# Packing the experts' leftover tokens four to a block instead of two in a mixture-of-experts layer

## The chip, the cores and the metric

The kernel runs on one core of one Trainium2 chip. The metric is the device time of one execution in microseconds (us): the median of several runs.

## What is computed

One decoder layer over 1024 tokens of width 1024, in float32: a mixer (a convolution group and a gated group, between two projections), LayerNorm, a two-level mixture of experts (MoE), and a gated LayerNorm. What the change touches is the MoE:

```python
g_p, g_idx = lax.top_k(g_probs, 1)                    # one of 4 groups
e_p, e_idx = lax.top_k(softmax(e_logits), 2)          # two of its 4 experts
expert_ids = g_idx * EXPERTS_PER_GROUP + e_idx
hidden = silu(x @ w_gate[e]) * (x @ w_up[e]) * combine[:, e]
y = sum over e of hidden @ w_down[e]
```

There are 16 experts, each with 1024 x 256 gate and up weights and 256 x 1024 down weights: 3 MB an expert. Each token goes to two experts, so there are 2048 (token, expert) pairs. With the inputs of the reference the experts get, in order, 88, 15, 27, 62, 451, 602, 461, 264, 17, 19, 10, 2, 13, 1, 9 and 7 tokens.

## The kernel before

**Stages.** The input projection and the convolutions come first, then the output projection with LayerNorm and the router (`choose`, `rank`: which expert, and which place in it, each token has), then a stretch in which the tokens are sorted into blocks, then the expert loop (line 1400), then the gate and the last LayerNorm (line 1485). Almost all multiplications split their operands into a high and a low part and run three passes (`mm3`). The order of work on every engine is written by hand (`manual_schedule`): what a queue is given first, it does first.

**Blocks.** An expert's tokens fill whole blocks of 128 rows; of what is left, over 64 tokens get a whole block too, and 1 to 64 get a half (`H` = 64 rows). With the counts above there are 16 whole blocks (1, 4, 5, 4 and 2 of experts 0, 4, 5, 6 and 7) and 12 rests of 64 rows. Blocks 0 to 15 (`NA`) are whole. Blocks 16 to 21 (up to `NS` = 22) hold two rests side by side, those of two experts: rest j takes columns 64j to 64j+63 of the array. These pair blocks run in plain float32, without the split. Blocks 22 and 23 run only where there are more rests than that (`plain_block`, in an `If`).

**Index work.** Lines 1143 to 1222, on VectorE, work out for every token its block and its row in it (`bf`, `qf`), make one-hot matrices `oh` (row, POOL, line 686) and `ohb` (block and half, line 1199), and one chain of small matmuls (line 1210) gives `idx`, the token for each row of each block. The expert of each unit goes into `ebi`, which SP reads as registers (`expert`, line 756).

**The loop** runs b = 0 to 13. Pass b multiplies whole block b+1 by gate and up (`gate_up`, two halves of 12 matmuls), turns block b+2 (`turn`), does block b's `down` (12 matmuls), splits the weights of block b+2 (ACT and DVE) and issues the loads for block b+3 on SP; these are conditional and move nothing when the block has the same expert (`changed`). Of the whole blocks that follow, 5, 10 and 14 have another expert than the one before.

**Pair steps** lie between these parts, one after each half of `gate_up` (from b = 1) and one or two (`EXTRA`) after `down`. A pair block has eight: `turn_plain`; four `pair_gu`; `pair_hid`; two `pair_down`. The six with weights issue four matmuls on 64 array columns each, 512 wide; the trace shows each as two records, so a weight step is eight records of 128 x 64 x 512. It reads two tiles of 512 KB, one of each expert.

**The ring** holds these tiles: four slots of two tiles. `load_pair` fills it, in the order of use: four slots ahead before the loop (line 1397), and after each weight step two tiles for the slot that the step has freed (`load_some`). They are issued on SP without condition, between the loads of the whole blocks and the stores of results (`store_y`), and SP takes all of these in order. The pool `rp` has 7 buffers: two for the down weights, two of the ring, the rest for `y`. Tokens are gathered by POOL.

Of the kernel before, what the change touches and what calls it, by code (L numbers as in the profile page):

```python
# [12 lines left out]
I32 = mybir.dt.int32  # L13
# [20 lines left out]
H = P // 2  # L34
NA = 16
NS = 22
# [9 lines left out]
def decoder_layer(ctx: ExitStack, tc: tile.TileContext, t: dict, out: bass.AP):  # L46
# [13 lines left out]
    rp = ctx.enter_context(tc.tile_pool(name="rp", bufs=7))  # L60
# [444 lines left out]
    pidx_m = const.tile([P, 1], F32, name="pidx_m")  # L505
    nc.gpsimd.iota(pidx_m, pattern=[[0, 1]], base=-1000, channel_multiplier=1, allow_small_or_imprecise_dtypes=True)
# [146 lines left out]
    def rank(t0, t1, weave=()):  # L653
# [16 lines left out]
        for step in (  # L670
# [4 lines left out]
            lambda: nc.vector.tensor_single_scalar(ri, si, 6, op=OP.logical_shift_right),  # L675
# [3 lines left out]
            next(weave, lambda: None)()  # L679
            step()  # L680
# [86 lines left out]
    def changed(b):  # L767
        return {"cond": expert(2 * b) != expert(2 * b - 2)} if b else {}

    def load_gu(b, part=range(4)):  # L770
        for q in part:
            fetch_gu(raw[q], expert(2 * b), q, **changed(b))

    def load_d(b):
        for k in range(2):
            fetch_d(rdn[k], expert(2 * b), k, **changed(b))
# [159 lines left out]
    def pair_gu(s, q):  # L936
# [3 lines left out]
        for k in range(2):  # L940
            for j in range(2):
                c = (2 * q + k) * P + j * H
                nc.tensor.matmul(pgu[b][j * H:(j + 1) * H, :], xgT[b][:, c:c + H],  # L943
                                 ring[(6 * s + q) % len(ring)][j].rearrange("p (m k f) -> p k m f", m=2, k=2)[:, k, :, :],
                                 start=q + k == 0, stop=q + k == 4)
# [3 lines left out]
    def pair_hid(s):  # L949
# [5 lines left out]
    def pair_down(s, k):  # L955
# [3 lines left out]
        for h in range(2):  # L959
            for j in range(2):  # L960
                c = k * P + j * H
                nc.tensor.matmul(pdn[b][h][j * H:(j + 1) * H, :], hTp[b][:, c:c + H],  # L962
                                 ring[(6 * s + 4 + k) % len(ring)][j][:, h * 512:(h + 1) * 512], start=k == 0, stop=k == 1)
# [3 lines left out]
    def plain_block(b):  # L967
        w4 = [*ring[0], *ring[1]]
        w4k = [a.rearrange("p (m k f) -> p m k f", k=2, m=2) for a in w4]
        src, xT = ring[2]  # L970
        gather(b, src)
        turn_plain(b, xT)
        for j in range(2):
            e = nc.sync.value_load(ebi[0:1, 2 * b + j:2 * b + j + 1], min_val=0, max_val=NE - 1)
# [66 lines left out]
    oh = line("oh")[:, 0:NT * H].bitcast(F16).rearrange("p (j t q) -> p j t q", j=2, q=H)  # L1041
# [83 lines left out]
    for h in range(2):  # L1125
# [24 lines left out]
        lambda: nc.vector.scalar_tensor_tensor(ci, count[0], float(H - 1), floor_, op0=OP.add, op1=OP.max),  # L1150
# [4 lines left out]
        lambda: nc.vector.tensor_scalar(odd0, pairs, -1.0, float(2 * NA), op0=OP.mult, op1=OP.add),  # L1155
        lambda: nc.vector.tensor_max(odd0, odd0, pairs),
# [9 lines left out]
    nc.vector.tensor_scalar(own[:, 0, :], cx[:, 0:NE], 2.0, pidx, op0=OP.mult, op1=OP.is_le)  # L1166
    nc.vector.scalar_tensor_tensor(wk, cs[:, 0:NE], -2.0, uo, op0=OP.mult, op1=OP.add)
    nc.vector.tensor_scalar(own[:, 1, :], cs[:, 0:NE], 2.0, pidx, op0=OP.mult, op1=OP.is_gt)
    nc.vector.scalar_tensor_tensor(wk, wk, 32.0, nf[:, 0:NE], op0=OP.mult, op1=OP.add)
    nc.vector.scalar_tensor_tensor(own[:, 2, :], nf[:, NE:], -1000.0, uo, op0=OP.mult, op1=OP.add)  # L1170
# [5 lines left out]
    nc.vector.scalar_tensor_tensor(own[:, 0, :], own[:, 2, :], pidx_m, own[:, 0, :], op0=OP.is_equal, op1=OP.add)  # L1176
# [13 lines left out]
    nc.vector.scalar_tensor_tensor(wf[:, 1, :], wf[:, 1, :], 2.0, hb, op0=OP.mult, op1=OP.is_le)  # L1190
    nc.vector.scalar_tensor_tensor(bf, wf[:, 0, :], 2.0, hb, op0=OP.mult, op1=OP.add)
# [5 lines left out]
    ebi = const.tile([1, 64], I32, name="ebi")  # L1197
    ohb = ebx[:, 256:256 + NT * 2 * NB].bitcast(F16).rearrange("p (c l b) -> p c l b", l=2, b=NB)
    nc.vector.tensor_tensor(
        ohb, iorow[:, 0:2 * NB].rearrange("p (b l) -> p l b", l=2)[:, None, :, :].to_broadcast([P, 2 * NT, 2, NB]),  # L1200
        bf[:, :, None, None].to_broadcast([P, 2 * NT, 2, NB]), op=OP.is_equal)
    nc.vector.tensor_copy(ebi[:, 0:2 * NB], pe[0:1, 0:2 * NB])
# [4 lines left out]
    todo = [(j, i) for i in range(NT) for j in range(2)]  # L1207
    for n, (j, i) in enumerate(todo):
        for l in range(2):
            ahead = nc.tensor.matmul(pix[l * H:(l + 1) * H, 0:NB], oh[:, j, i, :], ohb[:, j * NT + i, l, :],  # L1210
# [5 lines left out]
    nc.vector.tensor_scalar(ebi[:, 63:64], cs[0:1, 2 * NE - 1:2 * NE], odd0[0:1, :], None, op0=OP.add)  # L1216
# [346 lines left out]
```

## Time and profile before

| | |
|---|---|
| median of 3 runs | 733.39 us (732.62 to 735.53) |
| profiled execution, own time | 732.19 us |
| its span, first to last instruction | 730.4 us |
| TensorE matmuls (PE) busy | 708.3 us, 97% |
| VectorE (DVE), ScalarE (ACT), GpSimd (POOL) busy | 564.0, 332.4, 184.9 us |
| moved by DMA | 142.09 MB |

The loop with pair steps lies between about 403 and 604 us of the span. PE, DVE, ACT and POOL are engines; "PEld" is the loading of PE's weights; "SPq" is SP issuing a transfer. "gu" and "dn" are the outputs of gate/up and of down, "gT" a turned block, "hT" turned hidden values, "cv" and "rdn" the tiles that receive a whole block's weights, "ring" those of the rests. Line numbers are those of the kernel before.

### The profile page before, as it was taken

What the parts mean: (1) busy time and instruction counts of PE and PEld (TensorE: products, weight loads), DVE (VectorE), ACT (ScalarE), POOL (GpSimd) and SP (SyncE); (2) the same over time, 40 slices, a digit from 0 to 9 for tenths busy, and PEclk for the clock granted to TensorE, in tenths of its full rate; (3) what the DMA queues carried; (4) which work ended last, traced back from release to release, by engine and by line L of the source; (5) the groups of instructions that cost most, each with busy time, mean ns of one, the idle gap of its engine ahead of it and who ended that gap; (6) DMA issues with size and microseconds to landing.
All of it is one profiled execution on the core that took longest, in us unless ns stands there. A gap on an engine that the chain in (4) does not pass through costs nothing.

```text
span 730.4 us, 10338 instructions
## 1 busy us (share of the span) xinstructions
PE 708.3 (97%) x3558; PEld 537.3 (74%) x3558; DVE 564.0 (77%) x790; ACT 332.4 (46%) x544; POOL 184.9 (25%) x174
## 2 busy tenths in 40 slices
PE   6999999999999999999989999999999999999995
PEld 5898888888888888777767565665665666787874
DVE  6958999997985788998767656866556576788786
ACT  5761112324223733450357676767565675522220
POOL 3262122456363212135251110111011101621101
PEclk9999999999999999999999999999999999999999
DMA  8554111110111313452267899988888976887422
GB/s 311 207 210 156 57 57 35 54 57 30 58 58 51 123 58 116 139 179 87 116 235 272 329 402 387 358 310 322 301 331 318 385 257 238 280 305 243 173 90 84
DMA packets 40283, 142.09 MB, mean 195 GB/s; under 512 B 4610, under 2 KB 4738, under 8 KB 40228
## 3 DMA queue, kind: packets, MB, share of 16 engines
q1 hardware_dynamic: 33412, 116.95, 43.7%
q0 software_dynamic: 6672, 24.25, 9.6%
q8 instruction: 29, 0.48, 0.3%
q14 instruction: 26, 0.21, 0.1%
q10 hardware_dynamic: 144, 0.20, 0.1%
HBM read 149.77 MB, written 26.21 MB: 241 GB/s over the span
## 4 chain that ended last, share of the span: by engine, by line
PE 85%; DVE 5%; DMA 3%; issue 2%; POOL 2%; ACT 2%; SPq 0%; DVEq 0%; POOLq 0%; ACTq 0%
PE gu L943 6%; PE gu L94 4%; PE gu L96 4%; PE gu L95 4%; PE mix L555 4%; PE pg L1307 3%; PE mix L556 3%; PE mix L559 3%; PE pg L1308 3%; PE pg L1311 3%; PE dn L962 3%; PE gT L818 2%; PE c L263 2%; PE v L260 2%; PE v L259 2%
## 5 line engine op out<-in xcount | busy, mean ns | idle before, releaser
L283 DVE SCALAR_TENSOR_TENSOR cacc<-ab,tapT,cacc 128x1024 f32<-128x1024 f32 x116 | 149.6, 1290 | 10.9 <-ACT cacc L280 7.1
L91 DVE TENSOR_TENSOR el<-cv,eh 128x1024 fp32r<-128x1024 f32 x63 | 74.3, 1221 | 24.1 <-ACT eh L90 23.3
L143 POOL TENSOR_TENSOR wl<-wr,wh 128x1024 fp32r<-128x1024 f32 (+1 forms) x25 | 47.9, 1927 | 97.2 <-ACT wh L140 97.2
L809 POOL DMA_INDIRECT xg<-x_d,idx x22 | 25.7, 1170 | 178.1 <-PE gT L818 125.0
L140 ACT CAST wh<-wr 128x1024 fp32r<-128x1024 f32 x20 | 21.1, 1053 | 107.3 <-issue 35.0
L90 ACT CAST eh<-cv 128x1024 fp32r<-128x1024 f32 x63 | 62.9, 1052 | 0.0
L94 PE MATMUL gu<-eh,gh 128*128 128x512 f32 x128 | 53.2, 416 | 0.2 <-ACT gh L90 0.2
L555 PE MATMUL mix<-woh,ah 128*128 128x512 f32 x128 | 52.8, 413 | 0.0
L96 PE MATMUL gu<-eh,gl 128*128 128x512 f32 x128 | 50.2, 392 | 0.0
L556 PE MATMUL mix<-wol,ah 128*128 128x512 f32 x128 | 50.2, 392 | 0.0
L95 PE MATMUL gu<-el,gh 128*128 128x512 f32 x128 | 50.2, 392 | 0.0
L1307 PE MATMUL pg<-wgh,rh 128*128 128x512 f32 x120 | 48.2, 402 | 0.0
L1308 PE MATMUL pg<-wgl,rh 128*128 128x512 f32 x120 | 46.9, 391 | 0.1
L943 PE MATMUL gu<-ring,gx 128*64 128x512 f32 x192 | 45.6, 603 | 0.0
L187 POOL TENSOR_TENSOR rs<-ve,mhalf 128x1 f32<-128x1 f32 x16 | 17.4, 1090 | 95.9 <-DVE ve L186 95.9
L91 DVE TENSOR_TENSOR gl<-gT,gh 128x512 fp32r<-128x512 f32 x32 | 20.6, 685 | 26.7 <-ACT gh L90 26.7
L559 PE MATMUL mix<-woh,al 128*128 128x512 f32 x128 | 40.9, 390 | 0.0
L91 DVE TENSOR_TENSOR dl<-rdn,dh 128x1024 fp32r<-128x1024 f32 x32 | 37.8, 1220 | 2.6 <-ACT dh L90 1.3
L1311 PE MATMUL pg<-wgh,rl 128*128 128x512 f32 x120 | 37.7, 390 | 0.0
L90 ACT CAST dh<-rdn 128x1024 fp32r<-128x1024 f32 x32 | 32.2, 1060 | 0.0
L94 PEld LDWEIGHTS gu<-eh,gh 128*128 128x128 f32 x128 | 24.1, 188 | 11.1 <-issue 4.1
L259 PE MATMUL val<-xh,wh 128*128 128x256 f32 (+1 forms) x88 | 30.4, 346 | 0.0
(315 smaller groups left out, 1770.5 us busy)
## 6 DMA issues: line engine op xcount, KB each, us to landing
cv<-in_w_gu SPq DMA_DIRECT2D x60, 512.0 KB
ring<-in_w_gu SPq DMA_DIRECT2D x48, 512.0 KB
rdn<-in_w_down SPq DMA_DIRECT2D x32, 512.0 KB
ring<-in_w_down SPq DMA_DIRECT2D x24, 512.0 KB
ys_d<-y SPq DMA_DIRECT2D x22, 512.0 KB
wr<-in_w_in SPq DMA_DIRECT2D x20, 512.0 KB
wor<-in_w_out SPq DMA_DIRECT2D x8, 512.0 KB
y<-in_x SPq DMA_DIRECT2D x8, 512.0 KB
```

The costliest lines, as they stand in the source:

```text
L90: nc.scalar.copy(hi, src)
L91: (eng or nc.vector).tensor_sub(lo, src, hi.bitcast(F32))
L94: nc.tensor.matmul(o, ah, bh, start=start, stop=False)
L95: nc.tensor.matmul(o, ah, bl, start=False, stop=False)
L96: nc.tensor.matmul(o, al, bh, start=False, stop=stop)
L283: nc.vector.scalar_tensor_tensor(dst, abuf[c][:, j:j + SEQ], w, cacc[c], op0=OP.mult, op1=OP.add)
L555: nc.tensor.matmul(pmix[i][h], hi[:, ks], wh[:, s], start=k == 0, stop=False)
L556: nc.tensor.matmul(pmix[i][h], hi[:, ks], wl[:, s], start=False, stop=False)
L559: nc.tensor.matmul(pmix[i][h], lo[:, ks], wh[:, s], start=False, stop=k == NK - 1)
L943: nc.tensor.matmul(pgu[b][j * H:(j + 1) * H, :], xgT[b][:, c:c + H], ring[(6 * s + q) % len(ring)][j].rearrange("p (m k f) -> p k m f", m= ...
L1307: nc.tensor.matmul(pgt[i][h], hi[:, ks], wh[:, s], start=False, stop=False)
L1308: nc.tensor.matmul(pgt[i][h], hi[:, ks], wl[:, s], start=False, stop=False)
```

## The change

Rests come in units of 32 rows. An expert's rest of 1 to 32 tokens is one unit, of 33 to 64 two units of the same expert (over 64 a whole block, as before). Four units lie side by side in a block, 32 columns each, and there are four such blocks (16 to 19) for six; 20 to 23 stand in the `If`. The four units' tiles make a weight step of sixteen records of 128 x 32 x 512, which reads four tiles of 512 KB. The ring has ten single tiles (four of them now from `rp`, which gets 8 buffers), and after a weight step four loads are issued. A load of the ring carries the condition that the unit is in use. Index arithmetic changes accordingly; `ohb` becomes two arrays of 768 columns, one for each of a token's two choices, and the chain for `idx` has 64 matmuls of 32 columns for 32 of 64. `EXTRA` has six entries for nine and adds one step, not a second one, after `down`. Two more blocks of zeros are stored early. POOL's descriptor space is halved.

```diff
-H = P // 2
-NS = 22
+H = P // 4
+L = P // H
+NS = 20
-    rp = ctx.enter_context(tc.tile_pool(name="rp", bufs=7))
+    rp = ctx.enter_context(tc.tile_pool(name="rp", bufs=8))
...
-    def load_pair(s, n):
-        for j in range(2):
-            to, e = ring[(6 * s + n) % len(ring)][j], expert(2 * (NA + s) + j)
-            if n < 4:
-                fetch_gu(to, e, n)
-            else:
-                fetch_d(to, e, n - 4)
+    def held(s, n, j):
+        return ring[(L * (6 * s + n) + j) % len(ring)]
+
+    def load_quad(s, n, j):
+        u = L * (NA + s) + j
+        (fetch_gu if n < 4 else fetch_d)(held(s, n, j), expert(u), n % 4, cond=used > u)
...
-            for j in range(2):
+            for j in range(L):
                 c = (2 * q + k) * P + j * H
                 nc.tensor.matmul(pgu[b][j * H:(j + 1) * H, :], xgT[b][:, c:c + H],
...
-        lambda: nc.vector.tensor_scalar(ni[:, 1, :], ci, 6, 1, op0=OP.logical_shift_right, op1=OP.bitwise_and),
+        lambda: nc.vector.tensor_scalar(ni[:, 1, :], ci, 5, 3, op0=OP.logical_shift_right, op1=OP.bitwise_and),
         lambda: nc.vector.tensor_copy(nf, ni.rearrange("p a e -> p (a e)")),
+        lambda: nc.vector.tensor_scalar(nf[:, NE:], nf[:, NE:], 1.0, -1.0, op0=OP.max, op1=OP.add),
...
+    nc.vector.tensor_add(own[:, 0, :], own[:, 0, :], own[:, 2, :])
...
+    for j in range(2):
+        nc.vector.tensor_tensor(
+            ohb[j], iorow[:, 0:L * NB].rearrange("p (b l) -> p l b", l=L)[:, None, :, :].to_broadcast([P, NT, L, NB]),
+            bf[:, j * NT:(j + 1) * NT, None, None].to_broadcast([P, NT, L, NB]), op=OP.is_equal)
+        if j == 0:
+            nc.vector.tensor_copy(ebi[:, 0:L * NB], pe[0:1, 0:L * NB])
...
-    ring.append([line(f"ring{j}")[:, 0:D] for j in range(2)])
-    ring.extend([wide("ring", 2 * n + j)[:, 0:D] for j in range(2)] for n in range(2))
-    ring.append([R(f"ring{j}") for j in range(2, 4)])
+    ring.extend(line(f"ring{j}")[:, 0:D] for j in range(2))
+    ring.extend(wide("ring", j)[:, 0:D] for j in range(4))
+    ring.extend(R(f"ring{j}") for j in range(4))
...
-        for _ in range(done[0]):
+        for _ in range(L * done[0]):
             if loads:
-                load_pair(*loads.pop(0))
+                load_quad(*loads.pop(0))
...
-    EXTRA = (1, 2, 3, 4, 9, 10, 11, 12, 13)
+    EXTRA = (1, 3, 5, 7, 9, 11)
...
-        pair_some(2 if b in EXTRA else 1)
+        quad_some(1 if b in EXTRA else 0)
         load_some()
...
-    nc = _bacc.Bacc("TRN2", target_bir_lowering=False, num_devices=1)
+    nc = _bacc.Bacc("TRN2", target_bir_lowering=False, num_devices=1, dynamic_dma_scratch_size=8192)
```

## Rows read from the trace of the kernel before

**Rows 1.** The page: busy time of each engine over the span.
```profile
PE 708.3 (97%) x3558; PEld 537.3 (74%) x3558; DVE 564.0 (77%) x790; ACT 332.4 (46%) x544; POOL 184.9 (25%) x174
```

**Rows 2.** Waits of PE in the loop: who for whom, total, times, longest.
```profile
PE gT L818 <- ACT gx L933: 0.2, 1, 0.2
```

**Rows 3.** Windows of the loop: us, busy time per engine, clock, DMA share, GB/s.
```profile
397.50:403.50 6.00, 5.65 (x33) 4.43 (x32) 6.00 (x9) 6.00 (x10) 1.51 (x1) 1.00 0.74 236
403.50:598.20 194.70, 194.46 (x916) 118.47 (x915) 124.58 (x156) 127.32 (x191) 17.53 (x18) 1.00 0.90 338
403.50:413.40 9.90, 9.90 (x46) 5.58 (x45) 7.28 (x8) 5.44 (x8) 0.96 (x1) 1.00 1.00 387
428.80:445.10 16.30, 16.30 (x79) 9.79 (x80) 9.13 (x10) 11.64 (x17) 1.88 (x2) 1.00 1.02 406
445.10:460.50 15.40, 15.40 (x73) 9.36 (x74) 9.89 (x22) 11.84 (x17) 0.94 (x1) 1.00 1.01 388
521.00:534.70 13.70, 13.70 (x65) 8.75 (x65) 9.54 (x11) 9.14 (x14) 0.94 (x1) 1.00 0.87 301
566.40:582.80 16.40, 16.40 (x81) 9.89 (x80) 9.12 (x10) 10.89 (x17) 1.88 (x2) 1.00 1.00 395
```

**Rows 4.** Groups by line and form: the weight steps' matmuls, count, busy, mean.
```profile
L943 PE MATMUL gu<-ring,gx 128*64 128x512 f32 x192 | 45.6, 603 | 0.0
L962 PE MATMUL dn<-ring,hT 128*64 128x512 f32 x96 | 23.2, 605 | 0.0
```

**Rows 5.** The chain that ended last: start, us, what.
```profile
434.43 1.02 PE gT L932 x8
438.20 1.87 PE gu L943 x8
...
448.88 3.58 PE gu L943 x16
...
455.42 0.44 PE hT L847 x4
...
612.74 1.72 PE p L913 x4
...
617.86 2.94 DMA ys_d<-y
```

**Rows 6.** Timeline of PE at 359.6 us: the router's matmuls, then the next.
```profile
359.68 0.65 PE L605 MATMUL lg<-rT,wr 128*32 128x128 f32 x16
360.25 0.50 PE L94 MATMUL pp<-wp,ph 128*128 128x512 f32 x1
```

**Rows 7.** Timeline of SP: issues, first start to last end.
```profile
373.80 1.15 SPq L762 DMA_DIRECT2D cv<-in_w_gu  x2
397.59 5.53 SPq L762 DMA_DIRECT2D ring<-in_w_gu  x8
414.63 0.57 SPq L762 DMA_DIRECT2D cv<-in_w_gu  x2
415.42 0.93 SPq L765 DMA_DIRECT2D ring<-in_w_down  x2
```

**Rows 8.** Waits of SP in the loop, 403.5 to 598.2 us.
```profile
SPq L765 <- DVE dl L91: 28.8, 20, 3.2
SPq L762 <- DVE el L91: 17.8, 19, 2.2
```

**Rows 9.** Timeline of the index work, DVE and PE, 369 to 375 us.
```profile
370.24 0.96 DVE L1199 TENSOR_TENSOR ebx<-iorow,bf 128x768 f16<-128x768 f32 x1
371.96 0.68 PE L1210 MATMUL pix<-ebx,oh 128*64 128x24 f16 x32
373.32 1.22 DVE L91 TENSOR_TENSOR el<-cv,eh 128x1024 fp32r<-128x1024 f32 x1 [1.06 <-ACT eh L90]
374.47 0.17 DVE L1213 CAST idx<-pix 128x24 int32<-128x24 f32 x1
```

**Rows 10.** POOL, the first gather; and one window of low clock (Rows 3's columns).
```profile
375.49 4.82 POOL L809 DMA_INDIRECT xg<-x_d,idx  x1 [5.98 <-issue]
379.00:382.50 3.50, 3.50 (x10) 2.73 (x9) 0.38 (x2) 1.10 (x2) 2.90 (x3) 0.51 0.81 265
```

More of the change, by code (lines that the diff above doesn't have):

```diff
@@ L679, in rank @@
             next(weave, lambda: None)()
+            step()
+        for step in weave:
             step()
@@ L959, in pair_down @@
         for h in range(2):
-            for j in range(2):
+            for j in range(L):
                 c = k * P + j * H
                 nc.tensor.matmul(pdn[b][h][j * H:(j + 1) * H, :], hTp[b][:, c:c + H],
-                                 ring[(6 * s + 4 + k) % len(ring)][j][:, h * 512:(h + 1) * 512], start=k == 0, stop=k == 1)
+                                 held(s, 4 + k, j)[:, h * 512:(h + 1) * 512], start=k == 0, stop=k == 1)
         if k == 1:
@@ L967, in plain_block @@
     def plain_block(b):
-        w4 = [*ring[0], *ring[1]]
+        w4 = ring[0:4]
         w4k = [a.rearrange("p (m k f) -> p m k f", k=2, m=2) for a in w4]
-        src, xT = ring[2]
+        src, xT = ring[4:6]
         gather(b, src)
         turn_plain(b, xT)
-        for j in range(2):
-            e = nc.sync.value_load(ebi[0:1, 2 * b + j:2 * b + j + 1], min_val=0, max_val=NE - 1)
+        for j in range(L):
+            e = nc.sync.value_load(ebi[0:1, L * b + j:L * b + j + 1], min_val=0, max_val=NE - 1)
             rows = slice(j * H, (j + 1) * H)
@@ L1040, in decoder_layer @@
     short_split(0, (3,))
-    oh = line("oh")[:, 0:NT * H].bitcast(F16).rearrange("p (j t q) -> p j t q", j=2, q=H)
+    ohx = line("oh")
+    oh = ohx[:, 0:NT * H].bitcast(F16).rearrange("p (j t q) -> p j t q", j=2, q=H)
     for i in range(NT - 1):
@@ L1175, in decoder_layer @@
     nc.vector.tensor_mul(sb, o12.rearrange("p j t e -> p (j t) e"), wk[:, None, :].to_broadcast([P, 2 * NT, NE]))
-    nc.vector.scalar_tensor_tensor(own[:, 0, :], own[:, 2, :], pidx_m, own[:, 0, :], op0=OP.is_equal, op1=OP.add)
+    nc.vector.scalar_tensor_tensor(own[:, 2, :], uo, pidx, own[:, 2, :], op0=OP.is_le, op1=OP.mult)
     wi = small.tile([P, 2 * NT], I32, name="wi", bufs=1)
@@ L1196, in decoder_layer @@
     nc.tensor.matmul(pe[0:1, 0:P], ecol, ident, start=True, stop=True)
[L1197 to L1202, printed above, removed]
+    ebi = const.tile([1, L * NB + 1], I32, name="ebi")
+    ohb = [a[:, 256:256 + NT * L * NB // 2].bitcast(F16).rearrange("p (t l b) -> p t l b", l=L, b=NB)
+           for a in (ebx, ohx)]
+    for j in range(2):
[4 more added lines that the diff above has]
+            nc.vector.tensor_copy(ebi[:, 0:L * NB], pe[0:1, 0:L * NB])
     load_gu(1, (0,))
@@ L1206, in decoder_layer @@
     pix = bank("pix", "tr")
-    todo = [(j, i) for i in range(NT) for j in range(2)]
+    todo = [(j, i) for j in range(2) for i in range(NT)]
     for n, (j, i) in enumerate(todo):
-        for l in range(2):
-            ahead = nc.tensor.matmul(pix[l * H:(l + 1) * H, 0:NB], oh[:, j, i, :], ohb[:, j * NT + i, l, :],
+        for l in range(L):
+            ahead = nc.tensor.matmul(pix[l * H:(l + 1) * H, 0:NB], oh[:, j, i, :], ohb[j][:, i, l, :],
                                      start=n == 0, stop=n == len(todo) - 1)
@@ L1215, in decoder_layer @@
     gather(1)
-    nc.vector.tensor_scalar(ebi[:, 63:64], cs[0:1, 2 * NE - 1:2 * NE], odd0[0:1, :], None, op0=OP.add)
+    nc.vector.tensor_scalar(ebi[:, L * NB:], cs[0:1, 2 * NE - 1:2 * NE], odd0[0:1, :], None, op0=OP.add)
     split_gu(0, (2,))
@@ L1270, in gather_y @@
         for j in range(2):
-            part[i, j] = ring[3 - i % 3][j]
+            part[i, j] = ring[2 * (3 - i % 3) + j]
             at = slot[:, j * NT + i:j * NT + i + 1]
@@ L1372, in load_wg @@
     def load_wg(k):
-        wraw["g", k] = cv[k] if k < 4 else ring[k // 2 - 2][k % 2]
+        wraw["g", k] = cv[k] if k < 4 else ring[k - 4]
         (nc.gpsimd if k in (5, 7) else nc.sync).dma_start(wraw["g", k], w_pg[k * P:(k + 1) * P, :])
@@ L1397, in decoder_layer @@
     for _ in range(len(ring)):
-        load_pair(*loads.pop(0))
-    EXTRA = (1, 2, 3, 4, 9, 10, 11, 12, 13)
+        load_quad(*loads.pop(0))
+    EXTRA = (1, 3, 5, 7, 9, 11)
     for b in range(NA - 2):
@@ L1482, in decoder_layer @@
         split_wg(k)
-    g2, b2 = ring[0]
+    g2, b2 = ring[0:2]
     scale_r(1)
```

58 lines of the change are left out of this document (28 added, 30 removed).

## The prediction

> **What bounds the kernel now.** The page comes first: PE is busy for 97% of the span, the next engine for 77% [rows 1]. PE takes its work in order, so the question in each stage is whether it waits. For the loop, the view of waits has PE's one wait at 0.2 us in 194.7 us [rows 2]. So here the time is PE's own work, and work taken from PE comes off the end, as long as nothing else becomes late.
>
> What would be late next is in the windows. In the whole loop the 16 DMA engines are busy 0.90 of the time, and in four windows 1.00 to 1.02, at 387, 406, 388 and 395 GB/s [rows 3]. The transfers are nearly a second bound already. That decides this change: it takes time from PE and no bytes from the DMA.
>
> **What PE saves.** A weight step costs 1.87 us alone and 3.58 us for two in a row, so 0.16 us of each is the change to and from the narrow matmuls [rows 5]. A record of full width takes 1.72 / 4 = 0.43 us [rows 5], so eight on half of the columns would take 3.44 us in a line; 1.71 us says that the two halves run side by side. Before, there are 192 + 96 records [rows 4], that is 36 steps, four times two of them in a row (the chain has 3.58 us four times): 28 x 1.87 + 4 x 3.58 = 66.7 us (the groups' busy time says 68.8).
>
> Afterwards there are 24 steps, but of sixteen records on 32 columns. No such step with 512 columns is in the trace. Its bounds: four side by side, 16 x 0.43 / 4 + 0.16 = 1.88 us; only two, 3.44 + 0.16 = 3.60 us. The nearest row is the router's: sixteen records on 32 columns, with 128 columns of data, start at 359.68 and the next work starts at 360.25, 0.57 us later [rows 6]. In a line they would take 16 x 0.107 = 1.72 us; less 0.16 for the change it is 0.41 us, a quarter. So four run side by side, and I take 1.87 us: 24 x 1.87 = 44.9 us. The saving is 21.8 us, and with two turned blocks (1.02 each) and two turned hidden blocks (0.22 each) [rows 5] it is **24.3 us**.
>
> The Trainium skill, "TensorE: Matmul & The Clock Gate", section "Measured speedup vs the span model", gives 2.38 times for three column groups at 512 columns, not three; four at that efficiency would be 3.17 times, and a step an estimated 2.33 us instead of 1.87. By that rule the end would move by only the last six steps' share, 3 us, since the steps before wait for data anyway (below); the row at 359.68 speaks for the full four.
>
> **What the transfers take back.** Of the ring 13 units of six tiles are now fetched, 78 tiles, where before it was 72; two gathers and two stores of results fall away. In sum that is two transfers of 0.524 MB more. But 72 of the 78 tiles belong to the first three blocks, in 18 of the 24 steps, and each pass of the loop is shorter. So I count transfers against PE up to the last step that needs four tiles, the 18th, first step of pass 10.
>
> PE: a pass without steps is 9.7 us: 16.3 - 3 x 1.87 - 1.02 = 9.67; 13.7 - 2 x 1.87 - 0.22 = 9.74 [rows 3, 5]. By the new order, passes 1 to 9 hold 17 weight steps, three turned blocks and three turned hidden ones: 87.3 + 31.8 + 3.1 + 0.7 = 122.9 us, and 2.9 us of pass 10 lie ahead of the 18th step (12 of the 36 multiplications, 9.7 less the turn of 1.0). PE could be there 125.8 us after 403.5.
>
> Transfers: at 403.5 us some 1.4 MB of the first loads have come (6 us at 236 GB/s [rows 3]), so 7 of the ten tiles are outstanding. Then 62 tiles of the ring, 12 for two changes of expert, 12 gathers and 11 stores: 104. At the mean of the four full windows, 394 GB/s, one takes 1.33 us and all take 138.4 us. A lone transfer takes 2.94 us [rows 5], so the last lands 1.6 us after its turn: 140.0 us. PE waits for **14.2 us** there, in pieces from pass 2 on. Afterwards a step needs one tile, and PE is not held up. The ring cannot cover more: it holds two and a half steps ahead, and those tiles are in the count.
>
> Bounds: at the fullest window's 406 GB/s the wait is 10.1 us; at the whole loop's rate, 338 / 0.90 = 376 GB/s, it is 20.8 us. At 413 GB/s or more, or if part of the transfers can come after all that PE needs, it falls to 8 us and below.
>
> **Smaller terms.** *Index work.* DVE gets a step in `rank` and an addition (0.17 us each, as `idx`) and a second one-hot array of 0.96 us; PE gets 32 more small matmuls, 0.68 us [rows 9]. Between 0 and 2.0 us. The copy to `idx` stands behind a difference (`el`) that ends at 374.5 us because it waits for ACT; the second array would be done by about 373.3 and the matmuls by 373.9, so most is covered. I take 0.6 us. The other edits there replace one operation by one.
>
> *SP.* A load without condition costs SP 0.59 us (0.93 - 0.34), one with a condition that moves 0.80 (1.15 - 0.35), one that does not move 0.50 (0.57 - 0.07); the first reading of an expert's number adds some 0.5 (eight loads with two readings took 5.5) [rows 7]. In passes 1 to 9 that is 62 x 0.80 + 12 x 0.80 + 42 x 0.50 + 11 x 0.59 + 17 x 0.5, about 95 us of 140. It fits beside the transfers, and costs nothing as long as the DMA queue is not empty meanwhile. Behind each waiting load stand all later loads and the stores of `y`, and with two buffers for `y` ACT's copies wait for those stores; that cover is thin, and I keep 0 to 10 us for the range (see the rivals).
>
> *Others.* Two more stores of zeros lie in the convolutions, where transfers are few and PE has its data. Less descriptor space can make POOL wait: a gather's issue took 4.82 us once [rows 10]; POOL is busy 17.5 of 194.7 us in the loop [rows 3] and gathers run ahead, so nothing, with 3.9 us as the far end, for the one gather at the loop's end that work waits for. The eighth buffer of `rp` can only make loads earlier; before the loop PE's waits are for DVE and ACT: nothing, at best a gain of 0.5 us. PE's clock: while PE is busy it is granted in full; at 379 us, after PE had stopped for want of a bank, it fell to half, 1.2 GHz, for 3.5 us [rows 10]. Pauses of PE in the loop can do that again, at some 1.7 us each; it would lie mostly inside the waiting for data.
>
> **Sum.** -24.3 + 14.2 + 0.6 = -9.5 us. The profiled execution took 732.2 us (span 730.4): 722.7. The median is 1.2 us above it: **724 us**.
>
> **The rivals.**
>
> *No wait.* If the transfers run at over 413 GB/s or the ring's lead covers them, PE keeps its 24.3 us: 709.7, to 716 us. For it: PE did not wait once with the DMA at 1.02 for 16 us. Against: 104 transfers in 125.8 us are 433 GB/s, more than any window.
>
> *SP leaves the DMA empty; this one ends slower.* SP waits 46.6 us in the loop's 13 passes, mostly at loads that move nothing, for a difference on DVE to free a tile [rows 8]: 3.6 us a pass. If the new loads behind such a wait are late while the queue is empty, holes add to the 140 us: up to 9 x 3.6 = 32 us, the end at 756. From 9.5 us of holes on the change gains nothing, from 13 us on it is slower. For it: 95 + 32 us is most of 140. Against: four windows at 1.00 with the same waits in them. Holes of half the size would give 740; of 6 to 13 us, no difference.
>
> *The memory's share.* In one window the engines were 0.87 busy at 301 GB/s, so 346 GB/s when full [rows 3]. At that rate the wait is 33 us and the end 743. The Trainium skill, "HBM Reference", section "Specifications (TRN2)", gives an effective 358 GB/s for a core; the end would be at an estimated 738 us. The trace disagrees for this core alone, with 406 GB/s over 16 us.
>
> *Two groups side by side only.* 24 x 3.60 is 86 us, 20 more than before: PE is the bound again, the end at 751. Against it stands the row at 359.68.
>
> *The empty units are fetched after all.* Then 18 more tiles come in the last block's steps, 24 us of transfers in passes 9 to 13, which have few others: the same time.
>
> **How the numbers follow.** Forecast (719 to 729, the rates 406 to 380) 0.48; no wait 0.17; SP 0.21, 0.05 of it still a small gain, 0.09 no difference, 0.07 slower; memory's share 0.06; two groups 0.03; other 0.05. A measurement of this kernel can tell some 0.5%, 3.7 us, from no change. Faster than 729.7: 0.45 + 0.17 + 0.05 + 0.01 = 0.68; within 0.5%: 0.03 + 0.09 + 0.04 = 0.16; slower: 0.07 + 0.06 + 0.03 = 0.16. The range of 8 in 10 goes from 710, the full saving, to 736, the SP rival with 12 us of holes.
>
> **What would show it.** Right: 256 + 128 records of 128 x 32 x 512 on lines of the new steps, each mean still about 0.6 us; steps of 1.9 us in the chain; PE waiting for "ring" transfers, 10 to 20 us in all, in passes 2 to 9 and none after; DMA share near 1.0 up to about 545 us, then well below; the loop's end near 594 instead of 604 us. Wrong: steps of over 2.2 us; DMA share below 0.9 while PE waits for ring tiles (then SP is it, and its waits say for whom); no waits for ring tiles at all; a longer stretch from 370 to 385 us.

## The result, and the profile after

The change made the kernel slower: 744.92 us (median of 4 runs, 742.55 to 748.28) against 734.36 us for the kernel before in the same comparison, a ratio of 1.0152 with the 95% interval 1.0124 to 1.0179. The forecast was 724.0 us, in a range of 710 to 736. The profiled execution took 742.55 us, its span 740.8 us, 10.4 us more than before.

The page of the changed kernel: the busy time of the engines, the HBM line, and the group of the steps' gate/up matmuls (records, busy us, mean ns, idle us before them with what ended it).

```profile
PE 701.1 (95%) x3666; PEld 532.7 (72%) x3666; DVE 565.8 (76%) x791; ACT 326.4 (44%) x532; POOL 181.8 (25%) x171
...
HBM read 161.30 MB, written 26.21 MB: 253 GB/s over the span
...
L943 PE MATMUL gu<-ring,gx 128*32 128x512 f32 x256 | 43.7, 618 | 10.0 <-DMA ring<-in_w_gu 8.7
```

The steps are there in the number forecast, and in the chain one takes what it took before [rows 5] with twice the records:

```profile
542.93 1.85 PE gu L943 x16
```

So four column groups do run side by side. But PE now waits in the loop. The view of waits, PE from 403.5 to 607 us (where before it had one wait of 0.2 us [rows 2]):

```profile
PE gu L943 <- DMA ring<-in_w_gu: 8.7, 9, 2.5
PE gu L943 <- ACT gx L933: 1.3, 2, 1.0
PE gT L819 <- ACT gx L933: 0.5, 2, 0.3
PE dn L962 <- DMA ring<-in_w_down: 0.2, 1, 0.2
```

That is 10.7 us, and it is less than half of what PE loses in the loop (24.5 us against e_half, below). A step issues its matmuls in order of the tiles, and the wait for its second to fourth tile lies inside the group's "busy" time: 256 records cost 43.7 us here, and 31.0 us where the tiles are there in time (e_half, below).

Windows of the loop of the changed kernel (columns as in [rows 3]; the third from last is the clock, the second from last the DMA share):

```profile
403.50:556.60 153.10, 142.52 (x741) 83.86 (x741) 93.50 (x122) 92.72 (x136) 12.94 (x12) 0.99 0.96 368
415.00:427.00 12.00, 10.62 (x54) 5.78 (x54) 8.26 (x9) 6.77 (x10) 1.64 (x1) 1.00 0.84 295
455.00:465.00 10.00, 9.70 (x56) 6.12 (x52) 5.39 (x16) 7.23 (x12) 0.94 (x1) 1.00 0.69 239
465.00:515.00 50.00, 46.74 (x248) 27.81 (x241) 34.03 (x46) 32.49 (x49) 4.74 (x4) 0.97 0.99 378
515.00:556.60 41.60, 38.47 (x200) 21.90 (x201) 23.60 (x27) 23.05 (x33) 2.81 (x3) 1.00 1.00 394
```

In two stretches of 10 to 12 us in which PE waits the DMA is not full: its share is 0.84 and 0.69. What SP does there stands in its waits, 403.5 to 556.6 us, and in its timeline:

```profile
SPq L763 <- DMA ring<-in_w_gu: 12.1, 19, 1.2
SPq L766 <- DMA ring<-in_w_down: 8.5, 8, 1.9
SPq L766 <- DMA ring<-in_w_gu: 5.8, 6, 1.6
SPq L763 <- DMA ring<-in_w_down: 4.8, 7, 2.3
```

```profile
445.90 2.33 SPq L766 DMA_DIRECT2D rdn<-in_w_down  x2
449.36 0.34 SPq L855 DMA_DIRECT2D ys_d<-y  x1
450.73 5.39 SPq L763 DMA_DIRECT2D cv<-in_w_gu  x4
457.30 2.39 SPq L763 DMA_DIRECT2D ring<-in_w_gu  x3
```

Before, SP waited for differences on DVE [rows 8]; now it waits for transfers. The semaphore events of the trace say which: SP's issues use eight completion semaphores in turn, and each issue waits until the transfer eight issues back has landed. A load whose condition is false takes its turn like any other. The four loads of "cv" at 450.73 us move nothing (the block has the same expert), yet SP stands 5.4 us at them: the second goes out at 453.53 us, just after the ring load issued at 439.19 us, eight issues back, has landed (453.40). The first ring load behind them goes out at 457.30 us. Of the eight issues before it six moved nothing and one was a store, so the queue has run dry.

To see where the 10.4 us lie, I cut the executions at three places that PE's records give: the first turned block (first record of "gT"), the end of the last "down" of pass 13 (last "dn" record of that pass), and the third combined block (start of the third "rT"). From there on every execution takes 89.3 to 89.7 us.

| | first turned block at | from there to the end of pass 13 | from there to the third combined block | span |
|---|---|---|---|---|
| before | 384.6 | 219.2 | 37.3 | 730.4 |
| after | 385.9 | 221.2 | 44.2 | 740.8 |
| e_half | 385.7 | 196.7 | 42.6 | 714.5 |
| e_noskip | 385.4 | 204.6 | 45.2 | 724.8 |
| e_spread | 385.4 | 213.8 | 43.0 | 731.7 |
| e_tail | 386.1 | 222.7 | 43.1 | 741.3 |
| e_tf | 388.7 | 218.9 | 37.8 | 734.9 |
| e_sni | 384.9 | 200.2 | 43.4 | 718.0 |
| e_snif | 388.1 | 197.7 | 38.2 | 713.5 |

So +1.3 us before the loop, +2.0 in it where 10.1 less were forecast, and +6.9 behind it where nothing was.

### The profile page after: what moved, and what is told of

Read it like the earlier page. It is cut to its first block, busy times and chain, and to the rows that moved or that the text cites. A ratio compares the mean times of both kernels' runs of the same rounds, so it can differ in the third digit from the quotient of the medians.

```text
span 740.8 us, 10651 instructions
## 1 busy us (share of the span) xinstructions
PE 701.1 (95%) x3666; PEld 532.7 (72%) x3666; DVE 565.8 (76%) x791; ACT 326.4 (44%) x532; POOL 181.8 (25%) x171
## 2 busy tenths in 40 slices
DMA packets 40862, 144.22 MB, mean 195 GB/s; under 512 B 4674, under 2 KB 4802, under 8 KB 40804
## 3 DMA queue, kind: packets, MB, share of 16 engines
HBM read 161.30 MB, written 26.21 MB: 253 GB/s over the span
## 4 chain that ended last, share of the span: by engine, by line
PE 71%; DMA 13%; DVE 5%; ACT 4%; issue 3%; POOL 2%; SPq 1%; DVEq 0%; ACTq 0%; POOLq 0%
DMA ring<-in_w_gu 7%; PE pg L1313 4%; PE pg L1314 4%; PE pg L1317 4%; PE mix L554 4%; PE mix L555 3%; PE mix L558 3%; PE gu L95 2%; PE gu L943 2%; PE gu L96 2%; PE gu L97 2%; PE v L261 2%; PE c L261 2%; PE v L260 2%; PE c L264 2%
## 5 line engine op out<-in xcount | busy, mean ns | idle before, releaser
L943 PE MATMUL gu<-ring,gx 128*32 128x512 f32 x256 | 43.7, 618 | 10.0 <-DMA ring<-in_w_gu 8.7
L92 DVE TENSOR_TENSOR gl<-gT,gh 128x512 fp32r<-128x512 f32 x32 | 20.7, 685 | 24.5 <-ACT gh L91 24.1
L943 PEld LDWEIGHTS gu<-ring,gx 128*32 128x32 f32 x256 | 8.2, 110 | 36.8 <-DMA ring<-in_w_gu 20.0
L1279 POOL DMA_INDIRECT ring<-ys_d,slot x16 | 17.5, 1096 | 57.0 <-DMA ring<-in_w_pg 38.2
```

The costliest lines, as they stand in the source:

```text
L92: (eng or nc.vector).tensor_sub(lo, src, hi.bitcast(F32))
```

## The experiments

Ratios are against the kernel before on the same chip. "Loop" and "end" are the second and third stretch of the table.

### The loop: bytes, or holes in the queue

**e_half**: half of the ring's bytes, the same instructions. It leaves out half of each of the rests' weights and uses the other half twice.

```diff
-        (fetch_gu if n < 4 else fetch_d)(held(s, n, j), expert(u), n % 4, cond=used > u)
+        if n < 4:
+            fetch_gu(held(s, n, j), expert(u), n, slice(0, 512), cond=used > u)
+        else:
+            fetch_d2(held(s, n, j), expert(u), n % 4, cond=used > u)
```

> Only the first half of every ring tile is fetched, and the matmuls use it twice: the same instructions on PE and the same number of loads, but 78 transfers of 0.26 MB for 0.52 (the rests' results are then not the layer's). Theory (transfers and the holes in them): the waits for ring tiles fall from 26 us to under 6 us, the weight steps stay at 1.85 to 1.9 us, and the time is 719 to 726 us. Rival (SP's own issuing, some 95 us of work, or the steps themselves are the limit): waits of more than 12 us stay, and the time is above 731 us.

717.27 us, ratio 0.9779 (0.9734 to 0.9824), a little under the theory's range. No wait for the ring is left, and the groups of the steps:

```profile
L949 PE MATMUL gu<-ring,gx 128*32 128x512 f32 x256 | 31.0, 598 | 1.3 <-ACT gx L939 1.3
L968 PE MATMUL dn<-ring,hT 128*32 128x512 f32 x128 | 15.4, 598 | 0.0
```

46.4 us for 24 steps is 1.93 us a step. The loop takes 196.7 us, 22.5 less than before: the saving on PE is real, and SP's own time for its issues, all of which are still here, does not limit it.

**e_noskip**: the whole blocks' loads that move nothing are left out of the program.

```diff
-        for q in part:
+        for q in part if b in (0, 1, 5, 10, 14) else ():
```

> The whole blocks' loads that move nothing with these inputs (same expert as the block before) are left out of the program; every byte moved stays. Theory (holes): each of them takes a turn among the eight completion semaphores and holds SP until the transfer eight issues back has landed, so the queue runs empty behind it; without them PE's waits in passes 2 to 9 fall from 26 us to about 14 us and the time to 731 to 736 us. Rival (bytes alone): the queue is full anyway and the bytes are the same, so the waits stay at 24 to 27 us and the time at 742 to 746 us.

726.62 us, ratio 0.9909 (0.9883 to 0.9935); loop 204.6 us. The bytes moved are the same, and the time is 18 us less. A window of the loop, and SP in the stretch that stood at 0.69 above (it comes some 10 us earlier here):

```profile
441.00:530.00 89.00, 85.37 (x464) 51.71 (x463) 60.02 (x84) 60.46 (x89) 8.49 (x8) 1.00 1.03 413
```

```profile
447.17 1.47 SPq L766 DMA_DIRECT2D rdn<-in_w_down  x2
448.74 2.64 SPq L855 DMA_DIRECT2D ys_d<-y  x2
451.78 6.54 SPq L763 DMA_DIRECT2D ring<-in_w_gu  x6
```

The four loads of 5.39 us are gone. From 403.5 to 540 us the DMA moves 400 GB/s at a share of 1.00. From 407 to 419 us the share is 0.84 here too, but there PE does not wait: SP waits 6.8 us for PE to free a tile of a full ring. The gain is above what I expected, because I still took 14 us for the bytes. Against e_half the bytes cost 204.6 - 196.7 = 7.9 us, and the loads that move nothing cost 221.2 - 204.6 = 16.6 us. Each figure is from one execution; the kernels whose loop is that of the changed kernel (e_iol, e_end, e_tail, e_tf) take 218.9 to 222.7 us for it, so the 16.6 is known to some 3 us. The queue itself accounts for most of it: the 153.1 us at 368 GB/s above are 56.3 MB, which at 400 GB/s take 141 us, 12 us less.

**b_noskip**: the same edit in the kernel before.

> The kernel before, with the whole blocks' loads that move nothing left out of the program. Theory (holes cost only where PE waits for transfers): PE had no wait in the loop before, so nothing is gained: 732 to 735 us, ratio 0.997 to 1.002. Rival (the loads that move nothing cost time in themselves, in either kernel, and leaving them out is worth some 18 us anywhere): 715 to 722 us.

733.89 us, ratio 1.0003 (0.9982 to 1.0024). The same loads cost nothing before: there they hold SP too, but PE waits for nothing that SP brings.

**e_pool** and **e_poolcv** take one of the two kinds of loads to another queue, the ring's (e_pool) or the whole blocks' (e_poolcv).

```diff
-        nc.sync.dma_start(to[:, s], w_gu[bass.ds(e, 1), q, :, s].rearrange("e p f -> p (e f)"), **cond)
+        eng.dma_start(to[:, s], w_gu[bass.ds(e, 1), q, :, s].rearrange("e p f -> p (e f)"), **cond)
```

> Only the ring's loads are moved from SP to POOL's queue, whose completions go to other semaphores; the loads that move nothing stay on SP. Theory (holes): a ring load no longer stands behind a load that moves nothing, PE's waits in passes 2 to 9 fall from 26 to 14 us or less, and the time is 731 to 736 us. Rival (bytes alone): 742 to 746 us, as before the move. Second rival (POOL's price of an issue, near 0.94 us for a gather, and gathers standing behind loads that wait for a tile): waits for gathered tokens in place of ring tiles, 745 us or more.

> The changed kernel, with the whole blocks' loads from block 2 on issued by POOL in place of SP, those that move nothing among them; the ring's loads stay on SP. Nothing is tied to these inputs. Theory (holes): the loads that move nothing no longer take turns among the completion semaphores of the ring's loads, so most of what leaving them out gave is kept: 725 to 732 us. Rival (POOL): the gathers stand behind loads on POOL that wait for a split on DVE, and PE waits for gathered tokens: 740 us or more.

789.17 us and 787.52 us, ratios 1.0745 (1.0685 to 1.0805) and 1.0731 (1.0698 to 1.0763). In both the POOL rival came true: PE waits for gathered tokens, some 60 us in either. PE's waits in e_pool, 360 to 660 us, and POOL:

```profile
PE gT L932 <- DMA xg<-x_d,idx: 33.5, 3, 14.5
PE gT L819 <- DMA xg<-x_d,idx: 27.6, 6, 8.7
PE gu L943 <- DMA ring<-in_w_gu: 1.5, 1, 1.5
```

```profile
403.15 0.99 POOL L810 DMA_INDIRECT xg<-x_d,idx  x1 [0.41 <-issue]
424.96 0.57 POOL L763 DMA_DIRECT2D ring<-in_w_gu  x1 [20.82 <-PE gu L943]
```

A load that waits 20.8 us for its tile holds every gather behind it. A queue taken in order passes the wait on to whatever shares it; on POOL that is the gathers. Because these waits cover all else, the two runs do not say whether the ring's loads fare better without the empty turns; that rests on e_noskip and on the semaphore events.

**e_spread**: the third steps come in the later passes.

```diff
-    EXTRA = (1, 3, 5, 7, 9, 11)
+    EXTRA = (8, 9, 10, 11, 12, 13)
```

> The changed kernel with the six third steps in passes 8 to 13 in place of 1, 3, 5, 7, 9 and 11: the 18th weight step moves from pass 10 to pass 11 or later, and the early passes ask for less. Theory (PE outruns the transfers in the early passes): the waits for ring tiles fall from 26 to 10 to 16 us, and the last step lies behind the last product again, so that the end gains some 3 us too: 727 to 735 us. Rival (the holes come from SP's order wherever the steps lie): the waits stay at 22 us or more and the time at 738 us or more.

731.51 us, ratio 0.9958 (0.9931 to 0.9985). The loop falls to 213.8 us, so 17.1 us of the 24.5 us of waits stay (213.8 - 196.7). A later demand helps by a third, the rest stays. **e_soi** adds the order 0, 1, 3, 2 of the blocks (one of its lines is shown; tiles, gathers and loads follow the same order), and the edit of e_iol:

```diff
-    for s in range(NS - NA):
+    for s in (0, 1, 3, 2):
```

> The changed kernel with all its loads and nothing tied to these inputs: third steps in passes 8 to 13, the last quad (one unit used of four) worked as the third of four, unit numbers laid out as they are read. Theory (bytes asked for ahead of their time): with the light quad in the middle the demand falls under the supply in passes 7 to 10, and the last heavy quad has the whole end of the loop; PE waits for ring tiles under 8 us and the time is 722 to 729 us. Rival (the empty units' loads that move nothing now stand among the others, 18 more turns of the semaphores in the middle of the loop): new holes, 731 to 738 us.

730.75 us, ratio 0.9941 (0.9916 to 0.9967), loop 215.6 us: no better than e_spread. The time lies between the ranges of theory and rival, and whether new holes are the reason was not looked at. Executions of like kernels (e_spread, e_soi, e_sit, e_sif) lie at 212.0 to 215.6 us in the loop, so differences below some 3 us say nothing here.

### The stretch before the loop

**e_iol**: the unit numbers laid out in the order in which they are read.

```diff
+    unit = const.tile([P, L, NB], F32, name="unit")
+    nc.gpsimd.iota(unit, pattern=[[1, L], [L, NB]], base=0, channel_multiplier=0, allow_small_or_imprecise_dtypes=True)
...
-            ohb[j], iorow[:, 0:L * NB].rearrange("p (b l) -> p l b", l=L)[:, None, :, :].to_broadcast([P, NT, L, NB]),
+            ohb[j], unit[:, None, :, :].to_broadcast([P, NT, L, NB]),
```

> The changed kernel with the row of unit numbers laid out in the order in which the two one-hot comparisons read it (before and after the change it is read with a stride, of 2 and of 4 values). Theory (the stride of 4 makes the comparison slow): each takes 0.96 us or less in place of 1.54, the first gather starts some 1.2 us earlier, and the time is 742 to 744.5 us, 0.5 to 3 us less than the changed kernel. Rival (the time of the comparison is set by something else): 1.54 us each, no gain.

The timeline of DVE, first the changed kernel, then e_iol:

```profile
370.66 1.54 DVE L1204 TENSOR_TENSOR ebx<-iorow,bf 128x768 f16<-128x768 f32 x1
372.33 1.54 DVE L1204 TENSOR_TENSOR oh<-iorow,bf 128x768 f16<-128x768 f32 x1
```

```profile
370.85 0.96 DVE L1206 TENSOR_TENSOR ebx<-unit,bf 128x768 f16<-128x768 f32 x1
372.46 0.94 DVE L1206 TENSOR_TENSOR oh<-unit,bf 128x768 f16<-128x768 f32 x1
```

The stride is the cause of the longer comparison. The first turned block comes 0.6 us earlier. The measured 740.25 us, ratio 1.0074 (1.0051 to 1.0096), lie under the range expected and gain more than that over the changed kernel's 1.0152, which was taken on another chip. The trace accounts for 0.8 us of span only, and I count that; the rest is not explained.

### The end

**e_tail**: the first four gate weights are issued ahead of the last block's last step.

```diff
         next_gu(b + 2, (2, 3))
+        if b == NA - 3:
+            for k in range(4):
+                load_wg(k)
         gate_up(b + 1, NK // 2, NK)
...
-        if b == NA - 3:
-            for k in range(4):
-                load_wg(k)
```

> Theory (order on SP): the end lost 5 to 8 us because the last quad's store of results now stands ahead of the first four gate-weight loads on SP, which waits there for 7.8 us. With these four loads issued ahead of that step they start near 594 us instead of 604.5, the combined block is turned (rT) near 619 to 622 us instead of 627, and the time is 737 to 740 us. Rival (the loop's own lateness decides the end): rT stays near 625 to 627 us and the time at 743 to 746 us.

741.71 us, ratio 1.0101 (1.0040 to 1.0163). SP's timeline, the changed kernel, then e_tail:

```profile
595.85 8.55 SPq L855 DMA_DIRECT2D ys_d<-y  x2
604.50 2.20 SPq L1380 DMA_DIRECT2D cv<-in_w_pg  x4
```

```profile
597.54 0.33 SPq L855 DMA_DIRECT2D ys_d<-y  x1
599.71 4.82 SPq L1380 DMA_DIRECT2D cv<-in_w_pg  x4
605.76 0.33 SPq L855 DMA_DIRECT2D ys_d<-y  x1
```

The order on SP is mended, the first combined block comes 18.6 us after the last turned one instead of 23.8; but the end as a whole gains 1.1 us, and the time, 741.71 us, is in neither range. The second and third combined blocks now wait, for gathers that go out when the last store (`y` of block 15) has landed. By the semaphore events that store lands 5.1 us after its issue here, 4.1 in the changed kernel, 2.9 before.

Either wait brings a second loss. In the changed kernel PE's granted clock falls to half (0.50, 1.2 GHz) from 626.7 to 633.5 us, after PE had waited 3.9 us for the first combined block:

```profile
627.00:633.00 6.00, 5.90 (x17) 4.34 (x18) 4.36 (x7) 4.11 (x6) 2.79 (x3) 0.50 0.97 300
```

In e_tail it falls from 639.6 to 646.4 us, after the waits for the second and third. An estimated 3.4 us of the 6.8 are lost to the clock in each. In the same part of the kernel before, of e_tf and of e_snif (below) the clock stays in full.

**e_end** and **e_snit** (the same edit on e_sni) issue two loads that stood beside those stores ahead of them.

```diff
     split_last(0)
+    load_r(1)
+    load_wg(6)
     store_y(b, *ylast[b], (0,))
```

> The changed kernel with two edits at the loop's end alone: the gate-weight loads ahead of the last quad's step (as in e_tail), and the load of the next residual block and of gate weight 6 issued on SP ahead of the stores of the last two whole blocks instead of right behind them. Theory (the stores that the second gathers wait for land late because two more loads move beside them): the last store lands 2.5 to 3.5 us after its issue instead of 4.8, the second gathers start 2 us earlier, PE does not wait at the second and third combined blocks and its clock stays in full there; the third combined block is turned 41 to 43 us after the last whole block instead of 48, and the time is 735 to 739 us. Rival (those transfers are not what holds the store): 740 to 743 us as in e_tail.

> e_sni with the two loads (residual block 1, gate weight 6) ahead of the stores of the last two whole blocks. Theory: the end of e_sni loses 4 to 6 us after its loop to the late second gathers; with them on time the third combined block is turned 42 to 44 us after the last whole block instead of 49 and the time is 712 to 715 us. Rival: no change, 716 to 719 us.

740.54 us, ratio 1.0084 (1.0057 to 1.0110), and 719.16 us, 0.9797 (0.9773 to 0.9820); the ends take 43.0 and 43.8 us. This theory fell: the store is nearly as late without its neighbours (4.5 and 5.4 us). **b_scratch**, the kernel before with the descriptor space halved, excludes another part of the change:

```diff
-    nc = _bacc.Bacc("TRN2", target_bir_lowering=False, num_devices=1)
+    nc = _bacc.Bacc("TRN2", target_bir_lowering=False, num_devices=1, dynamic_dma_scratch_size=8192)
```

> The kernel before with one part of the change alone: POOL's descriptor space halved. Theory (the shortened space makes the gathers of the results late): behind the loop a gather's issue takes 1.6 us or more instead of 0.95, the second and third combined blocks are turned 12.5 to 14 us after the one before instead of 11.9 and 10.4, PE waits there and its clock falls to half, and the time is 735 to 740 us. Rival (the space costs nothing): the same times of issue, 732 to 735 us, ratio 0.998 to 1.002.

733.91 us, ratio 0.9992 (0.9974 to 1.0011): the space costs nothing, and the first gather takes 4.82 us with half of it as with all of it [rows 10].

**e_tf** (on e_tail) and **e_snif** (on e_sni) add instructions on PE, more than 200 us ahead of that store.

```diff
     pp(len(pp_steps))
+    fill = bank("fill", "tr")
+    for _ in range(62):
+        nc.tensor.matmul(fill[0:H, 0:NB], oh[:, 0, 0, :], ohb[0][:, 0, 0, :], start=True, stop=True)
```

> e_tail with the same 62 matmuls, otherwise the changed kernel. Theory (the end's loss has two parts, the gate weights behind the last step's store and the piece of PE's program on the last store): with both mended the third combined block is turned 41 to 43 us after the last whole block in place of 46.9 in e_tail and 48.0 in the changed kernel, and the time is 734 to 738 us. Rival: 740 to 743 us as in e_tail.

> e_sni with the same 62 matmuls: now the store falls midway between two pieces of PE's program. Theory: it lands under 3.5 us after its issue in place of 5.0, PE does not wait at the second combined block, the third is turned 43 to 45 us after the last whole block in place of 49.1, and the time is 711 to 715 us. Rival: 717 to 720 us, the end as in e_sni.

737.89 us, ratio 1.0048 (1.0018 to 1.0077), and 714.61 us, ratio 0.9725 (0.9688 to 0.9763). The DMA view over the last store's time, by queue (packets, MB, share), in e_sni and in e_snif:

```profile
q1 hardware_dynamic: 450, 1.65, 89.3%
q8 instruction: 1, 0.02, 1.9%
q14 instruction: 1, 0.01, 0.5%
```

```profile
q1 hardware_dynamic: 221, 0.77, 73.3%
q14 instruction: 1, 0.01, 0.9%
```

and POOL, the gathers behind it, in the same two kernels (start, time, what it had waited for):

```profile
604.89 1.65 POOL L1281 DMA_INDIRECT ring<-ys_d,slot  x1 [12.40 <-DMA ys_d<-y]
```

```profile
603.75 0.98 POOL L1284 DMA_INDIRECT ring<-ys_d,slot  x1 [10.59 <-DMA ys_d<-y]
```

With the piece of the program (q8) out of the way the store lands 3.2 us after its issue instead of 5.0, PE does not wait for the second combined block, and the end falls from 43.4 to 38.2 us; in e_tf the store lands in 3.7 us instead of 5.1, and the end falls from 43.1 to 37.8, half a microsecond from the kernel before. These ends are of one execution each; the intervals of the ratios overlap (e_tail with e_tf, e_sni with e_snif). That q8 is PE's program is inferred from its pace, one piece after every 206 to 293 of PE's instructions in the loop of e_sni. The Trainium skill ("Runtime: NRT & Kernel Launch", "Instruction fetch mechanics") has programs refilled by DMA in blocks of 16 KiB, 256 instructions, at a cost that is mostly hidden; the trace agrees on the block, and in these two pairs of runs its cost was not hidden. The first turned block comes 2.6 and 3.2 us later in the two, but not in e_sif (below), so what the matmuls cost there is open.

A rival has to be set beside this: the 62 matmuls also move the last two stores against each other (issued 1.53 us apart in e_sni, 2.19 in e_snif; 1.36 in e_tail, 0.67 in e_tf). Two other runs hold that still. SP's issue of the two stores, and the one next, in b_scratch and in e_spread:

```profile
618.13 1.71 SPq L854 DMA_DIRECT2D ys_d<-y  x2
620.04 0.32 SPq L1382 DMA_DIRECT2D c<-x_d  x1
```

```profile
611.78 1.71 SPq L855 DMA_DIRECT2D ys_d<-y  x2
613.66 0.32 SPq L1388 DMA_DIRECT2D c<-x_d  x1
```

With no piece of q8 beside it the last store lands in 3.2 us (b_scratch), with one that starts 1.4 us after its issue in 5.0 us (e_spread). So the piece goes with some 1.8 us at the same spacing. But it is not what delayed the store in the changed kernel itself: there the piece ran from 623.92 to 625.12 us and the store was issued at 625.08, only 0.42 us behind the one before it, where the kernel before had 2.15 us between them.

**b_fill**, the 62 matmuls in the kernel before, was to bring the piece onto the store there.

> The kernel before with 62 small matmuls added on PE where it has little to do (ahead of the first turned block; their result is read by nobody). Theory (PE's program is fetched by DMA in pieces of 16 KB, one after every 255 to 260 of its instructions; in the kernel before, the last whole block's store falls midway between two pieces, in every kernel with the change so far on one, and the store then lands late): 124 more instructions on PE bring a piece onto that store; it lands 4.5 us or more after its issue in place of 2.9, the third combined block is turned 46 us or more after the last whole block in place of 43.0, and the time is 735 to 740 us. Rival (the store is late for another reason, in the change itself): an end as before, 732 to 735 us.

739.57 us, ratio 1.0055 (1.0030 to 1.0081), in the theory's range by luck: the piece came at 623.7 us, 2.4 us before the store's issue, the store landed in 2.9 us and the end took 37.6 us, as before. Most of the time went before the loop (first turned block at 390.6). The reverse of the effect is not shown. In **e_sit** (e_spread, e_iol and the edit of e_end) and **e_sif** (e_spread, e_iol and the 62 matmuls) nothing is tied to these inputs:

> The same as e_snit with all conditional loads kept, so that nothing is tied to these inputs: third steps in passes 8 to 13, unit numbers as they are read, the two loads ahead of the stores. Theory: the loop as in e_spread (the last whole block turned near 593 us), the end 4 to 6 us shorter: 724 to 728 us, ratio to the kernel before 0.986 to 0.992. Rival (the end does not gain): 729 to 733 us.

> The changed kernel with nothing tied to these inputs: third steps in passes 8 to 13, unit numbers as they are read, the 62 matmuls. Theory: the loop of e_spread and e_sit (last whole block turned at 591 to 594 us) and an end without the late store, 724 to 727 us. Rival: 729 to 732 us.

729.42 us, ratio 0.9958 (0.9935 to 0.9982), and 730.36 us, 0.9924 (0.9896 to 0.9952): in both the rival's range held. e_sit's end is still 41.8 us, e_sif's 39.6; there the store takes 4.3 us with no piece of PE's program beside it, so that piece is not the only thing that can delay it. The two last stores are 0.81 us apart there; that this spacing is the reason is not shown.

### The two causes of waits together

**e_sni**: the edits of e_spread, e_noskip and e_iol.

> The changed kernel with three edits that paid alone: third steps in passes 8 to 13, the whole blocks' loads that move nothing left out of the program (tied to these inputs), unit numbers laid out as they are read. Theory (the two causes of ring waits are separate and both go): waits for ring tiles under 4 us in the loop, the last whole block turned at 578 to 582 us as with half the bytes, and a time of 714 to 719 us. Rival (what is left is bytes alone, 14 us as forecast, and spreading only moves it): 721 to 726 us.

717.97 us, ratio 0.9762 (0.9736 to 0.9787); loop 200.2 us, 3.5 from e_half with all the bytes moved. With the matmuls of e_snif it is the best version: 714.61 us, 2.7% under the kernel before, for inputs with these changes of expert. Without that tie, e_sif gains 0.8%.

## Why the prediction was wrong, point by point

- **PE's saving: right.** Forecast 24.3 us with steps of 1.87 us; without waits the loop is 22.5 us shorter (e_half), with steps of 1.93. By the Trainium skill's 2.38 times for three groups ("TensorE: Matmul & The Clock Gate", "Measured speedup vs the span model") a step would have taken an estimated 2.33 us; the trace disagrees, four groups ran fully side by side.
- **The transfers' bytes: right in kind, too dear.** Forecast 14.2 us, measured 7.9 us (e_noskip against e_half). The count was right: 136.5 us at 400 GB/s are 54.6 MB, 104 transfers. The prediction set PE at the 18th step, free of waits, 125.8 us after 403.5, and the transfers at 140.0. That step, in e_noskip and in e_half:

```profile
539.51 1.92 PE L962 MATMUL dn<-ring,hT 128*32 128x512 f32 x16
```

```profile
531.92 1.92 PE L968 MATMUL dn<-ring,hT 128*32 128x512 f32 x16
```

So it came after 136.0 us with all bytes, 4.0 us sooner than forecast, and after 128.4 us without the waits, 2.6 us later. The rate of the four full windows was too low a guide: in e_noskip 89 us in a row ran at 413 GB/s, the rate for which the prediction's own bounds give a wait of 8 us. The estimate by the Trainium skill's 358 GB/s ("HBM Reference", "Specifications (TRN2)") is not borne out: windows with a share of 1.00 and more ran at 387 to 415 GB/s, before [rows 3] and after. That figure is a core's share when both cores of a pair stream; the same section has a core streaming alone at about 425 GB/s, and the traces of this one core agree with that far better.
- **SP: the step that failed.** "It fits beside the transfers, and costs nothing as long as the DMA queue is not empty meanwhile", put at 0, cost 16.6 us (after against e_noskip). The rival "SP leaves the DMA empty" had the place and the sign, and its 0 to 32 us hold the size; but it priced the wait for a difference on DVE, and what holds SP is the turn of a load that moves nothing, behind the transfer eight issues back. The count that was missing is not SP's time (95 us of 140, which fits: e_half keeps every issue and has no wait for the ring) but the loads in flight: of eight turns up to six in a pass were empty. The four full windows of before that spoke against the rival had the same waits, in a stretch where nothing depended on them.
- **The end: not in the sum at all.** The term is 0 and was +6.9 us. That the last step moves from behind the last product to between the halves of `gate_up`, and with it the store that SP takes ahead of the gate weights, stood in the order of steps and was not followed past the loop. By this the first combined block came 20.0 us after the end of pass 13 instead of 15.0; the other 1.9 us came behind it, where PE ran at half clock for 6.8 us. The late last store and the piece of PE's program on it cost time only in the kernels in which that order is mended (e_tail, e_spread, e_sni); they could not have been read from the trace of before as a cost.
- **Index work.** Forecast 0.6 us, measured 1.3: the second one-hot array was taken at 0.96 us, from a row with another stride, and both took 1.54. PE also stopped 3.8 us for the first gather (before: 1.0), and its clock then fell to half for 6.8 us, from 384.3 us on, where before it did for 3.4 us, from 379.0 on [rows 10]. Windows of the changed kernel:

```profile
384.00:388.00 4.00, 2.06 (x9) 1.87 (x10) 0.32 (x1) 0.67 (x2) 0.00 (x0) 0.54 0.99 366
388.00:392.00 4.00, 4.00 (x12) 3.09 (x12) 3.42 (x4) 2.39 (x3) 0.94 (x1) 0.60 0.97 377
```

Against the forecast the sum is: saving +1.8, bytes -6.3, holes +16.6, end +6.9, start +0.7, in all +19.7; the forecast of -9.5 became +10.4, a miss of 19.9. What was to show a wrong forecast did: a DMA share of 0.69 and 0.84 while PE waits, "then SP is it".

## What to carry to other kernels

When a queue's loads become what the bound engine waits for, count its conditional loads as turns, moved or not: they bound how many real transfers are in flight, and a profile in which nothing waits for them shows them as free. Moving loads to another queue moves their waits too, so first name what is queued behind them there. And follow a moved step past the end of the loop it sits in: here 6.9 us were lost there, 5.0 of them ahead of the first combined block, where one store had changed places with four loads.

## What was unexpected of the hardware

- The profile's HBM line counts the loads that move nothing as reads. e_noskip leaves out 66 of 0.524 MB, 34.6 MB; its HBM read is 126.70 MB against 161.30, 34.60 less, while the DMA packets' bytes are the same (144.17 against 144.22 MB).

```profile
HBM read 126.70 MB, written 26.21 MB: 211 GB/s over the span
```

- The same comparison of 128 x 768 values took 0.96 us with an operand read in order and with a stride of two values (before, [rows 9]), 1.54 us with a stride of four.
- A single 16 KB piece of an engine's program beside a 512 KB store goes with that store landing 5.0 us instead of 3.2 after its issue (e_spread and b_scratch, e_sni and e_snif), and in e_sni, through the gather behind it, with 5 us of the kernel's end. The reverse was tried once (b_fill) and missed the store, so it is not proven as the cause.
